# The shift's share of the keys as VectorE dot products with transposed key weights, and the shift's own products in pairs of k tiles

## Chip, cores and metric

One core of one Trainium2 chip. The metric is the device time of one launch in microseconds (us). The kernel before took a median of 1557.75 us over 3 runs (1557.66 to 1557.91).

## What is computed

One layer of a diffusion backbone on 256 latent tokens x and 256 context tokens ctx, 2048 features, all in float32. What matters here is the first half:

```
mod   = silu(c)     @ w_mod + b_mod          # shift, scale, gate, ... for x
mod_c = silu(c_ctx) @ w_mod + b_mod          # the same for ctx
h  = rms_norm(x,   g) * (1 + scale)   + shift
hc = rms_norm(ctx, g) * (1 + scale_c) + shift_c
q, k, v, gates = h @ w_in ;   k_c, v_c = hc @ w_in
```

There are ten key heads (eight of the neighbourhood mixer, two of the windowed one) of 128 features each. Attention, gates, branch and output projections, a second norm and a gated convolutional FFN follow. Because the shift is the same vector for all tokens of a stream, its share of a key head is one vector of 128 numbers per stream: shift @ w_k. The kernel makes the keys without the shift and adds that vector afterwards.

## The kernel before

All products are float32 products in two or three parts: a weight block of 1 MB (128 partitions x 2048) is loaded by `raw_block` (line 97) into one of four buffers of the tag "raw", and `halves` (line 116) splits it into `wh` on ScalarE (line 109) and `wl` on VectorE (line 113), two instructions each, into two buffers each. `block(ahead)` (line 144) hands out the next block of the stream, asks for the split of the block after it and for the loads of one or more further ones. The framework's scheduler lays out each engine's instructions in order of the program among those it holds ready, so a later load or product can be put ahead of an earlier one that isn't ready; once laid out, the order on an engine is fixed.

The stages around the change, in order:

- First sweep of the keys (lines 319 to 340): six key heads, sixteen k tiles, each used as soon as its scale column is there. At its end the sums are evacuated by VectorE, six instructions at line 340, and the accumulators become free.
- Second sweep (lines 345 to 363): the other four key heads. Ahead of the 24 key products of each k tile stand the products of the shift itself, silu(c) @ w_mod, in `pm` (line 354): four column tiles of 32 columns with 512 moving columns. Their weights `wm_sh` come through the four "raw" buffers, two tiles ahead, beside the key weights. Then ScalarE evacuates `pm` (line 365), TensorE transposes it (368), VectorE adds the bias to make the columns `shc` (373), and ScalarE and VectorE make the whole of h, hi and lo part, from the normalised input `xn` (lines 377 to 385). Then the pool that holds `xn` is closed (386).
- Values (lines 388 to 449): ten weight blocks, 576 products at line 428. Beside them `key_shift` (line 402) loads the key weights a second time, 640 KB for each k tile, and multiplies them with `shc` on TensorE, four column tiles per k tile, in `pc` (line 409). After the ninth block `pc` is evacuated, transposed (439) and copied, and 20 ScalarE instructions (445) add it to the keys. Also beside the values, thirteen modulation columns are made by `mods` (line 176): a load of 1 MB of `wm_b` and one VectorE dot product over 2048 columns (line 186), with the row silu(c) broadcast to all partitions in `crb` (line 189).
- Attention (lines 451 to 591): query blocks are made two heads ahead by `fill` (line 494), beside rotation, scores, softmax and values. The mask is in `bz` (line 395), which is loaded at the start of the values.
- Gates and branches (lines 593 to 636): one dot product beside most gates, and one more beside the branch block of j = 4 and j = 8 (line 623). The remaining six of the 48 modulation columns come beside the output projection.

Then come the output projection (line 640), the FFN (from line 773) and the down projection.

Of the kernel before, what the change touches and what calls it, by code (L numbers as in the profile page):

```python
# [15 lines left out]
P = 128  # L16
D = 2048
KT = D // P
S = 256
# [12 lines left out]
# columns of the packed per-feature vectors  # L32
# [10 lines left out]
# blocks of the weight stream, in the order of use  # L43
# [7 lines left out]
NK1 = 6  # key tiles of the first sweep  # L51
# [5 lines left out]
def layer_kernel(ctx, tc, xc, xt, ccol, crow, wm_sc, wm_sh, wm_b, cols, wk, ws, rope, mask_a, bias_b, out):  # L57
# [34 lines left out]
    ggd = tc.dram_tile([2, KT, P], F32, name="ggd")  # L92

# [3 lines left out]
    def raw_block(src, shape=(P, 2048)):  # L97
        nraw[0] += 1
        r = wp.tile([P, 2048], F32, tag="raw", bufs=4, name=f"raw{nraw[0]}")
# [25 lines left out]
    # the weight stream: loads run two or three blocks ahead, the splitting one  # L125
# [5 lines left out]
    raws, parts, nblk, place, queue, last = {}, {}, [0], {}, {}, []  # L131

    def load_to(i):
        for q in range(min(i, len(srcs) - 1) + 1):
            if q not in raws:
                raws[q] = raw_block(*srcs[q])
# [14 lines left out]
    def mm2(pt, wh, wl, act, k0, n, kk0, first, last, step=P, off=0):  # L151
        """accumulate n k-tiles; act is [P, kt, 2(hi, lo), 256]; result: two halves to be added"""
# [23 lines left out]
    def mods(n, row, ahead=1):  # L176
        """the next n modulation columns of x: one dot product per partition"""
# [11 lines left out]
    def silu_row(pool):  # L189
        r = pool.tile([P, D], F32, tag="crb", bufs=1, name=f"crb{nmod[0]}")  # L190
# [16 lines left out]
    def gain_dram(i, g):  # L207
        """as a row"""
# [9 lines left out]
    def keep_busy(n, nm):  # L218
        """products of constants: the tensor engine's clock falls when it waits for long"""
# [4 lines left out]
    # ================= mixers =================  # L224
    zs = ExitStack()
    with ExitStack() as mx:
# [3 lines left out]
        with ExitStack() as at:  # L230
# [3 lines left out]
            def rope_of(t, which, nm):  # L234
                """in place; the pairs of the rotation lie 64 partitions apart"""
# [10 lines left out]
            shc = hcp.tile([P, KT, 32], F32, name="shc")  # L246
# [11 lines left out]
            nc.gpsimd.memset(shc, 0.0)  # L258
            rsc = {}

# [11 lines left out]
            # (1 + b) g of the scale  # L272
# [71 lines left out]
            # the other keys, while the weights of the shift come in  # L344
            pm = bank("pmsh")
            pk = [acc(f"pk{NK1 + i}") for i in range(NK2)]
            rsh = {k: raw_block(wm_sh[k]) for k in range(2)}
            for g in range(4):
                wh, wl = block(1)
                for k in range(4 * g, 4 * g + 4):  # L350
                    if k + 2 < KT:
                        rsh[k + 2] = raw_block(wm_sh[k + 2])
                    for j in range(4):
                        nc.tensor.matmul(  # L354
                            pm[32 * j : 32 * j + 32, :], cc[:, k, :], rsh[k][:, 512 * j : 512 * j + 512],
                            start=k == 0, stop=k == KT - 1)
                    for v in range(2):
                        x_ = xn[:, k, v * S : v * S + S]
                        nc.vector.scalar_tensor_tensor(
                            out=x_, in0=x_, scalar=Gc[:, k, v : v + 1], in1=rs[:, v * S : v * S + S],  # L360
                            op0=ALU.mult, op1=ALU.mult)
                    for i in range(NK2):
                        keys(pk[i], wh, wl, (k % 4) * NK2 * P + i * P, k)
            ev = sp.tile([P, 512], F32, tag="hf", bufs=2, name="evsh")
            nc.scalar.activation(ev[:], pm[:], AF.Copy)
# [3 lines left out]
            # pt[p, b, 32 j + v] is the value of feature (4 j + b) * 128 + p  # L369
            view = pt[:].rearrange("p (b j w) -> p j b w", b=4, j=4, w=32)  # L370
            bm = col[:, C_BMOD : C_BMOD + KT].rearrange("p (j b) -> p j b", j=4)
            for v in range(2):
                nc.vector.tensor_tensor(
                    out=shc[:].rearrange("p (j b) w -> p j b w", j=4)[:, :, :, v],
                    in0=view[:, :, :, v], in1=bm, op=ALU.add)
            # the whole of h
# [17 lines left out]
            # what is added to the scores, and one row of zeros for the context  # L394
            bz = vp.tile([P, 7, S], F32, name="bz")
            crb = silu_row(cbp)
            sync.dma_start(out=bz[:, 0:2], in_=mask_a)
            nc.gpsimd.memset(bz[:, 6], 0.0)
            pc = bank("pc")
            nkc = [0]  # L400

            def key_shift(n):
                for _ in range(n):
                    k = nkc[0]
                    nkc[0] += 1
                    r = raw_block(wk[k], (P, KW))
                    for j in range(4):
                        n_ = min(384, KW - 384 * j)
                        nc.tensor.matmul(
                            pc[32 * j : 32 * j + 32, :n_], shc[:, k, :], r[:, 384 * j : 384 * j + n_],  # L410
                            start=k == 0, stop=k == KT - 1)

            nb = 0
            for c, (n0, nw, per) in enumerate(((0, 512, 4), (512, 512, 4), (1024, 256, 8))):
                pv = [acc(f"pv{c}_{i}") for i in range(4)]
                for g in range(KT // per):
                    wh, wl = block(2)
                    for kk in range(per):
                        if nb < 8 and kk % 2:
                            key_shift(1)  # L420
                        if kk in (0, 3, 6) and nb and (kk != 3 or nb > 7):
                            mods(1, crb[:])
# [9 lines left out]
                    if nb == 9:  # L432
                        ev = cbp.tile([P, 384], F32, tag="evk", name="evk")
                        nc.gpsimd.memset(ev, 0.0)
                        nc.scalar.activation(ev[:, :P], pc[:, :P], AF.Copy)
                        nc.scalar.activation(ev[:96, P:], pc[:96, P:384], AF.Copy)
                        pt = bank("ptk")
                        for b in range(3):
                            nc.tensor.transpose(pt[:, b * P : b * P + P], ev[:, b * P : b * P + P], ident[:])
                        kb = cbp.tile([P, 384], F32, tag="kb", name="kb")  # L440
                        nc.vector.tensor_copy(kb[:], pt[:, :384])
                        for i in range(NKVA + NHB):
                            for v in range(2):
                                o_ = (i % 3) * P + 32 * (i // 3) + v
                                nc.scalar.activation(
                                    kT[:, i, v * S : v * S + S], kT[:, i, v * S : v * S + S], AF.Identity, bias=kb[:, o_ : o_ + 1])
# [10 lines left out]
            # query blocks and the first gates are done beside the attention of earlier heads  # L457
# [36 lines left out]
            def fill(half):  # L494
                """half of the products of the next query (or gate) block"""
# [113 lines left out]
        for j in range(KT):  # L609
# [13 lines left out]
            mods(1 if j in (4, 8) else 0, crb[:])  # L623
# [63 lines left out]
    def rstd_tok(ss, r):  # L687
        """the sum of the first three parts is ready when the last part comes"""
# [9 lines left out]
    with ExitStack() as ys:  # L698
# [19 lines left out]
        # second norm: shift with its bias, gain times (1 + scale)  # L718
# [80 lines left out]
    # the first two pairs go k by k, as h2 comes  # L799
# [9 lines left out]
    # behind the products of a block: its halves are added before the next block but one is split,  # L809
    # the rest of its work comes after that  # L810
# [172 lines left out]
```

## Time and profile before

| | us |
|---|---|
| median of 3 runs | 1557.75 (1557.66 to 1557.91) |
| span of the profiled execution, first to last instruction | 1556.1 |
| TensorE busy | 1540.4 (99%) |
| VectorE busy | 1067.3 (69%) |
| ScalarE busy | 783.8 (50%) |
| end of the first sweep / of the second sweep / of the values | 102.4 / 165.9 / 296.6 |

The profiled execution shows its span and no other time of its own; the median lies 1.65 us above that span. Engines are PE (TensorE), PEld (its weight loads), DVE (VectorE), ACT (ScalarE), POOL (GpSimd) and SP (the queue that issues the loads). A line such as "L409" is a line of the kernel. Matmul records are pipelined, so a matmul that is shown as 0.40 us long may be followed by the next after 0.23 us: costs are read from one start to the next.

### The profile page before, as it was taken

Reading aid. Unit: us, or ns where it says so; the run is one execution under the profiler, and the core shown is the slowest. Engines: PE = TensorE matmul, PEld = TensorE weight load, DVE = VectorE, ACT = ScalarE, POOL = GpSimd, SP = SyncE. Lnnn points to the kernel's source line nnn. Section 1 sums busy time; section 2 is a strip of 40 time slices with the busy share of each in tenths; the row PEclk is TensorE's granted clock in tenths of the full one; section 3 lists DMA queues with packets and bytes.
Section 4 is the critical chain, followed back from the end, with each engine's and each line's share of the span. In section 5 each row is a group of like instructions: output and inputs, shape, how many; then the busy total and the mean of one; then the engine's idle time right before and its main releaser. Section 6 shows DMA issues by size and latency. Waiting matters only on the chain.

```text
span 1556.1 us, 22874 instructions
## 1 busy us (share of the span) xinstructions
PE 1540.4 (99%) x9181; PEld 1317.5 (85%) x9181; DVE 1067.3 (69%) x1611; ACT 783.8 (50%) x1291; POOL 23.8 (2%) x29
## 2 busy tenths in 40 slices
PE   8999999999999999999999999999999999999998
PEld 8987766989998888888888888888888888888886
DVE  3563633798878898887667878887888776444444
ACT  4431411677775454555467555555555554343332
POOL 2210000000000000000000000000000000000000
PEclk9999999999999999999999999999999999999999
DMA  9868787733337898887955666666666556555552
GB/s 371 324 263 324 261 316 266 270 114 138 136 145 295 319 344 329 327 303 281 366 191 197 241 238 244 243 226 234 244 244 229 204 190 254 206 189 190 189 189 81
DMA packets 58393, 377.97 MB, mean 243 GB/s; under 512 B 6384, under 2 KB 6448, under 8 KB 16176
## 3 DMA queue, kind: packets, MB, share of 16 engines
q1 hardware_dynamic: 57712, 375.47, 64.9%
q8 instruction: 72, 1.18, 0.3%
q10 hardware_dynamic: 576, 1.05, 0.2%
q14 instruction: 33, 0.27, 0.0%
HBM read 372.27 MB, written 4.22 MB: 242 GB/s over the span
## 4 chain that ended last, share of the span: by engine, by line
PE 97%; DMA 1%; ACT 1%; DVE 0%; POOL 0%; SPq 0%; issue 0%; DVEq 0%; POOLq 0%
PE pu L156 21%; PE py_d L653 16%; PE pu L157 11%; PE pv L428 7%; PE pk L311 7%; PE pg L156 7%; PE py_o L653 6%; PE pq L156 4%; PE pb L156 4%; PE pg L157 4%; PE pq L157 2%; PE pb L157 2%; PE po L564 1%; PE s L534 1%; PE pmsh L354 1%; PE pm L282 1%
## 5 line engine op out<-in xcount | busy, mean ns | idle before, releaser
L113 DVE TENSOR_TENSOR wl<-raw,wh 128x1024 fp32r<-128x1024 f32 (+2 forms) x470 | 555.6, 1210 | 334.8 <-ACT wh L109 324.0
L109 ACT ACTIVATE wh<-raw 128x1024 fp32r<-128x1024 f32 (+2 forms) x470 | 474.2, 1042 | 410.2 <-PE py_d L653 135.5
L156 PE MATMUL pu<-h,wh 128*128 128x512 f32 x1408 | 488.6, 390 | 0.0
L157 PE MATMUL pu<-h,wl 128*128 128x256 f32 x1408 | 396.8, 282 | 0.0
L156 PEld LDWEIGHTS pu<-h,wh 128*128 128x128 f32 x1408 | 264.3, 188 | 55.6 <-ACT h L768 0.3
L157 PEld LDWEIGHTS pu<-h,wl 128*128 128x128 f32 x1408 | 266.1, 189 | 0.1
L653 PE MATMUL py_d<-wh,ff 128*128 128x512 f32 x704 | 221.1, 395 | 0.0
L156 PE MATMUL pg<-hx,wh 128*128 128x512 f32 x464 | 161.5, 390 | 0.0
L653 PEld LDWEIGHTS py_d<-wh,ff 128*128 128x128 f32 x704 | 131.9, 187 | 32.2
L186 DVE SCALAR_TENSOR_TENSOR raw<-raw,crb 128x2048 f32<-128x2048 f32 x64 | 146.1, 2285 | 16.9 <-DMA raw<-in_wm_b_dram 12.4
L653 PE MATMUL py_d<-wl,ff 128*128 128x512 f32 x352 | 139.0, 395 | 0.0
L157 PE MATMUL pg<-hx,wl 128*128 128x256 f32 x464 | 130.8, 282 | 0.0
L161 ACT ACTIVATE half_u<-pu 128x256 f32<-128x256 f32 x88 | 33.5, 383 | 152.8 <-PE pu L157 152.8
L156 PE MATMUL pq<-hx,wh 128*128 128x512 f32 x304 | 108.4, 395 | 0.0
L156 PEld LDWEIGHTS pg<-hx,wh 128*128 128x128 f32 x464 | 87.1, 188 | 18.3
L156 PE MATMUL pb<-oab,wh 128*128 128x512 f32 x256 | 89.6, 392 | 0.0
L157 PEld LDWEIGHTS pg<-hx,wl 128*128 128x128 f32 x464 | 87.7, 189 | 0.0
L311 PE MATMUL pk<-hx,wh 128*128 128x256 f32 x320 | 85.5, 290 | 0.2 <-PE pmsh L354 0.2
L157 PE MATMUL pq<-hx,wl 128*128 128x256 f32 x304 | 85.6, 282 | 0.0
L311 PE MATMUL pk<-hc,wh 128*128 128x256 f32 x320 | 82.8, 281 | 0.0
L653 PE MATMUL py_o<-wh,zz 128*128 128x512 f32 x256 | 80.3, 395 | 0.0
L653 PEld LDWEIGHTS py_d<-wl,ff 128*128 128x128 f32 x352 | 66.0, 187 | 16.3
(177 smaller groups left out, 1994.1 us busy)
## 6 DMA issues: line engine op xcount, KB each, us to landing
raw<-in_ws_dram SPq DMA_DIRECT2D x222, 1024.0 KB, 4.8
raw<-in_wm_b_dram SPq DMA_DIRECT2D x64, 1024.0 KB, 4.8
raw<-in_wm_sc_dram SPq DMA_DIRECT2D x16, 1024.0 KB, 7.6
raw<-in_wm_sh_dram SPq DMA_DIRECT2D x16, 1024.0 KB, 6.4
raw<-in_wk_dram SPq DMA_DIRECT2D x16, 640.0 KB, 5.0
raw<-in_wk_dram SPq DMA_DIRECT2D x7, 768.0 KB, 5.6
raw<-in_wk_dram SPq DMA_DIRECT2D x4, 1024.0 KB, 5.9
crb<-sild SPq DMA_DIRECT2D x4, 1024.0 KB, 5.9
```

The lines of the kernel that those rows point to most:

```text
L109: a_ = nc.scalar.activation(hi, src, AF.Copy)
L113: v_ = nc.vector.tensor_tensor(out=lo, in0=src, in1=hi, op=ALU.subtract)
L156: nc.tensor.matmul(pt[:, :], wh[:, w], a, start=first and i == 0, stop=False, skip_group_check=True)
L157: nc.tensor.matmul(pt[:, :S], wl[:, w], a[:, 0], start=False, stop=last and i == n - 1, skip_group_check=True)
L161: a_ = nc.scalar.activation(t[:], pt[:, S:], AF.Copy)
L186: nc.vector.scalar_tensor_tensor(out=r, in0=r, scalar=1.0, in1=row, op0=ALU.mult, op1=ALU.mult, accum_out=modx[:, j : j + 1])
L282: nc.tensor.matmul(pm[32 * j : 32 * j + 32, :P], cc[:, q, :], r[:, q * P : q * P + P], start=q < 4, stop=q >= KT - 4)
L311: nc.tensor.matmul(pk[:, v * S : v * S + S], wt[:, w], hh[v][:, k, a], start=k == 0 and a == 0 and wt is wh and v == 0, stop=k == KT - 1 a ...
L354: nc.tensor.matmul(pm[32 * j : 32 * j + 32, :], cc[:, k, :], rsh[k][:, 512 * j : 512 * j + 512], start=k == 0, stop=k == KT - 1)
L428: nc.tensor.matmul(pv[i][:, :nw], src[:, k, a, t0 : t0 + P], wt[:, w], start=k == 0 and q == 0, stop=k == KT - 1 and q == 2)
L534: nc.tensor.matmul(s_ps[:], qs[hd][:, a, qt * P : qt * P + P], k_[:], start=q == 0, stop=q == 2)
L653: nc.tensor.matmul(py[t][:], act[:, k, a, t * P : t * P + P], wt[:, w], start=k == 0 and q == 0, stop=k == nk - 1 and q == 2)
```

## The change

Three things are changed (comments that were taken out are not shown):

1. The shift's products run two k tiles at a time. Four `wm_sh` loads are asked for at once, and the key weights of the second sweep (blocks 9 to 12) get one buffer of their own in the pool of `xn`. The bias is added on evacuation (a loaded row `brow`, on VectorE, in place of the ScalarE copy), the shift rows are written to DRAM (`shd`), and `shc` is copied from the transposes.
2. `key_shift` and all that hangs on `pc` are gone. In their place stand 20 dot products on VectorE (`beside`): for each of the ten key heads one load of transposed key weights `wkt` (1 MB) and one product for each of the two streams, with the shift row broadcast to all partitions (`shr`). Two ScalarE additions per head follow at once (`key_bias`). They run beside value blocks 2 to 7; after them come eleven modulation columns, whose row takes over the buffer of a shift row.
3. The mask's buffer `bz` is made and loaded after the values, and two modulation columns move to the branch blocks of j = 11 and j = 13.

```diff
+            home.update({q: sp for q in range(9, 13)})
...
-            rsh = {k: raw_block(wm_sh[k]) for k in range(2)}
...
+            rsh = {k: raw_block(wm_sh[k]) for k in range(4)}
+            for k in range(KT):
+                if k % 4 == 0:
+                    wh, wl = block(1)
+                if k % 2 == 0:
+
+                    for q in (k, k + 1):
+                        for j in range(4):
+                            nc.tensor.matmul(
+                                pm[32 * j : 32 * j + 32, :], cc[:, q, :], rsh[q][:, 512 * j : 512 * j + 512],
+                                start=q == 0, stop=q == KT - 1)
+                    for q in (k + 4, k + 5):
+                        if q < KT:
+                            rsh[q] = raw_block(wm_sh[q])
...
-            nc.scalar.activation(ev[:], pm[:], AF.Copy)
+            nc.vector.tensor_tensor(out=ev[:], in0=pm[:], in1=brw[:], op=ALU.add)
+            sync.dma_start(out=shd.rearrange("j w n -> (j w) n"), in_=ev)
...
+            shr = []
+            for v in range(2):
+                shr.append(cbp.tile([P, D], F32, tag="row", bufs=2, name=f"shr{v}"))
+                sync.dma_start(
+                    out=shr[v].rearrange("p (j n) -> p j n", j=4), in_=shd[:, v].partition_broadcast(P))
+            junk = cbp.tile([P, D], F32, name="junk")
+            kb = cbp.tile([P, NKVA + NHB, 2], F32, name="kb")
+            rkt = {0: raw_block(wkt[0])}
+            crb = [None]
+            nbeside = [0]
+
+            def key_bias(i):
+                for v in range(2):
+                    o_ = slice(v * S, v * S + S)
+                    nc.scalar.activation(kT[:, i, o_], kT[:, i, o_], AF.Identity, bias=kb[:, i, v : v + 1])
+
+            def beside(n):
                 for _ in range(n):
-                    k = nkc[0]
-                    nkc[0] += 1
-                    r = raw_block(wk[k], (P, KW))
-                    for j in range(4):
-                        n_ = min(384, KW - 384 * j)
-                        nc.tensor.matmul(
-                            pc[32 * j : 32 * j + 32, :n_], shc[:, k, :], r[:, 384 * j : 384 * j + n_],
-                            start=k == 0, stop=k == KT - 1)
+                    i, v = divmod(nbeside[0], 2)
+                    nbeside[0] += 1
+                    if i < NKVA + NHB:
+                        if v == 0 and i + 1 < NKVA + NHB:
+                            rkt[i + 1] = raw_block(wkt[i + 1])
+                        r = rkt[i]
+                        nc.vector.scalar_tensor_tensor(
+                            out=r if v else junk[:], in0=r, scalar=1.0, in1=shr[v][:], op0=ALU.mult, op1=ALU.mult,
+                            accum_out=kb[:, i, v : v + 1])
+                        if v:
+                            key_bias(i)
+                    else:
+                        if crb[0] is None:
+                            crb[0] = silu_row(cbp, "row", 2)
+                        mods(1, crb[0][:])
...
-                        if nb < 8 and kk % 2:
-                            key_shift(1)
-                        if kk in (0, 3, 6) and nb and (kk != 3 or nb > 7):
-                            mods(1, crb[:])
+
+                        if nb and kk < (3 if nb % 2 else 4):
+                            beside(1)
...
+            bzp = at.enter_context(tc.tile_pool(name="bzp", bufs=1, side="right"))
+            bz = bzp.tile([P, 7, S], F32, name="bz")
+            sync.dma_start(out=bz[:, 0:2], in_=mask_a)
+            nc.gpsimd.memset(bz[:, 6], 0.0)
...
-            mods(1 if j in (4, 8) else 0, crb[:])
+            mods(1 if j in (4, 8, 11, 13) else 0, crb[:])
```

The transposed weights and the bias row are laid out ahead of the launch: `o["wkt"] = np.concatenate([kb, ka], axis=1).T.reshape(NKVA + NHB, P, D)` and `o["brow"]`.

## Rows read from the trace of the kernel before

**Rows 1.** The page: engines' busy time, the chain by engine, the splits on VectorE.

```profile
PE 1540.4 (99%) x9181; PEld 1317.5 (85%) x9181; DVE 1067.3 (69%) x1611; ACT 783.8 (50%) x1291; POOL 23.8 (2%) x29
...
PE 97%; DMA 1%; ACT 1%; DVE 0%; POOL 0%; SPq 0%; issue 0%; DVEq 0%; POOLq 0%
...
L113 DVE TENSOR_TENSOR wl<-raw,wh 128x1024 fp32r<-128x1024 f32 (+2 forms) x470 | 555.6, 1210 | 334.8 <-ACT wh L109 324.0
```

**Rows 2.** Busy by stretch: span, then PE, PEld, DVE, ACT, POOL, clock, DMA share, GB/s.

```profile
18.00:30.00 12.00, 11.85 (x164) 11.04 (x166) 5.71 (x11) 6.77 (x13) 2.90 (x2) 1.00 0.97 388
182.00:297.00 115.00, 115.00 (x645) 87.22 (x644) 52.14 (x48) 32.58 (x54) 0.67 (x2) 1.00 0.79 295
297.00:312.00 15.00, 15.00 (x85) 12.93 (x84) 12.10 (x24) 11.70 (x18) 0.00 (x0) 1.00 0.57 216
540.00:560.00 20.00, 20.00 (x117) 17.67 (x117) 19.66 (x26) 10.95 (x17) 0.00 (x0) 1.00 0.96 370
```

**Rows 3.** TensorE in order of time around one of the key shift's products.

```profile
205.90 0.40 PE L428 MATMUL pv<-wh,hx 128*128 128x512 f32 x1
206.23 0.85 PE L409 MATMUL pc<-raw,shc 128*32 128x384 f32 x8
207.00 0.50 PE L428 MATMUL pv<-wh,hx 128*128 128x512 f32 x1
207.34 0.40 PE L428 MATMUL pv<-wl,hx 128*128 128x512 f32 x1
207.57 0.40 PE L428 MATMUL pv<-wh,hx 128*128 128x512 f32 x1
```

**Rows 4.** The tile pc: its products (start of the first and the last).

```profile
L409 PE MATMUL pc<-raw,shc x128: 272/486/510, 167.1 to 270.3; 128*32 128x384 f32 x96, 128*32 128x128 f32 x32
```

**Rows 5.** TensorE at the start of the values, and at the transposes of pc.

```profile
165.92 0.60 PE L368 MATMUL ptsh<-ident,evsh 128*128 128x128 f32 x4
167.08 0.85 PE L409 MATMUL pc<-raw,shc 128*32 128x384 f32 x8 [0.57 <-DVE shc L373]
168.34 0.50 PE L428 MATMUL pv<-wh,hx 128*128 128x512 f32 x1 [0.41 <-ACT hx L383]
...
284.93 0.49 PE L439 MATMUL ptk<-ident,evk 128*128 128x128 f32 x3
285.18 0.48 PE L428 MATMUL pv<-wh,hx 128*128 128x256 f32 x2
```

**Rows 6.** TensorE in the second sweep: the first shift products, then a later one.

```profile
102.48 2.78 PE L354 MATMUL pmsh<-raw,cc 128*32 128x512 f32 x24
105.41 0.36 PE L311 MATMUL pk<-hx,wh 128*128 128x256 f32 x1 [0.15 <-PE pmsh L354]
...
157.81 0.28 PE L311 MATMUL pk<-hc,wl 128*128 128x256 f32 x1
158.02 1.06 PE L354 MATMUL pmsh<-raw,cc 128*32 128x512 f32 x8
...
159.24 0.28 PE L311 MATMUL pk<-hc,wh 128*128 128x256 f32 x1
```

**Rows 7.** VectorE in order of time: dot products at the start and end of the values.

```profile
189.43 2.29 DVE L186 SCALAR_TENSOR_TENSOR raw<-raw,crb 128x2048 f32<-128x2048 f32 x1 [4.40 <-DMA crb<-sild]
191.65 0.08 DVE L186 DVE_READ_ACCUMULATOR raw<-raw,crb 128x1 f32 x1
...
293.06 2.29 DVE L186 SCALAR_TENSOR_TENSOR raw<-raw,crb 128x2048 f32<-128x2048 f32 x1
```

**Rows 8.** Loads issued from 182 to 297 us: count, KB each, median us to landing.

```profile
raw<-in_wm_b_dram SPq DMA_DIRECT2D x12, 1024.0 KB, 6.6
crb<-sild SPq DMA_DIRECT2D x1, 1024.0 KB, 6.9
```

**Rows 9.** SP's queue after the second sweep: the issue of the broadcast row silu(c).

```profile
182.45 0.42 SPq L191 DMA_DIRECT2D crb<-sild  x1
```

**Rows 10.** Waits from 300 to 312 us: us in total, times, longest.

```profile
ACT q L109 <- DVE rq L241: 1.4, 1, 1.4
```

More of the change, by code (lines that the diff above doesn't have):

```diff
@@ L56, in layer_kernel @@
 @with_exitstack
-def layer_kernel(ctx, tc, xc, xt, ccol, crow, wm_sc, wm_sh, wm_b, cols, wk, ws, rope, mask_a, bias_b, out):
+def layer_kernel(ctx, tc, xc, xt, ccol, crow, wm_sc, wm_sh, wm_b, cols, wk, wkt, ws, brow, rope, mask_a, bias_b, out):
     nc = tc.nc
@@ L92, in layer_kernel, with raw_block @@
     ggd = tc.dram_tile([2, KT, P], F32, name="ggd")
+    shd = tc.dram_tile([4, 32, 512], F32, name="shd")
     nraw = [0]
     nmod = [0]
-    def raw_block(src, shape=(P, 2048)):
+    def raw_block(src, shape=(P, 2048), pool=None):
         nraw[0] += 1
-        r = wp.tile([P, 2048], F32, tag="raw", bufs=4, name=f"raw{nraw[0]}")
+        r = (pool or wp).tile([P, 2048], F32, tag="raw", bufs=1 if pool else 4, name=f"raw{nraw[0]}")
         n = int(np.prod(shape[1:]))
@@ L130, in layer_kernel @@
     srcs += [(ws[i], (P, 2048)) for i in range(NBLK)]
-    raws, parts, nblk, place, queue, last = {}, {}, [0], {}, {}, []
+    raws, parts, nblk, place, home, queue, last = {}, {}, [0], {}, {}, {}, []
     def load_to(i):
@@ L135, in load_to @@
             if q not in raws:
-                raws[q] = raw_block(*srcs[q])
+                raws[q] = raw_block(*srcs[q], pool=home.get(q))
     def split_to(i):
@@ L187, in mods, with silu_row @@
                 out=r, in0=r, scalar=1.0, in1=row, op0=ALU.mult, op1=ALU.mult, accum_out=modx[:, j : j + 1])
-    def silu_row(pool):
-        r = pool.tile([P, D], F32, tag="crb", bufs=1, name=f"crb{nmod[0]}")
+    def silu_row(pool, tag="crb", bufs=1):
+        r = pool.tile([P, D], F32, tag=tag, bufs=bufs, name=f"crb{nmod[0]}")
         sync.dma_start(out=r, in_=sild.rearrange("a b -> (a b)").partition_broadcast(P))
@@ L345, in layer_kernel @@
             pm = bank("pmsh")
+            brw = sp.tile([P, 512], F32, tag="sq", bufs=2, name="brw")
+            sync.dma_start(out=brw, in_=brow)
             pk = [acc(f"pk{NK1 + i}") for i in range(NK2)]
-            rsh = {k: raw_block(wm_sh[k]) for k in range(2)}
[L348 to L352, printed above, removed]
-                    for j in range(4):
-                        nc.tensor.matmul(
-                            pm[32 * j : 32 * j + 32, :], cc[:, k, :], rsh[k][:, 512 * j : 512 * j + 512],
-                            start=k == 0, stop=k == KT - 1)
[L357 to L363, printed above, removed]
@@ L364, in layer_kernel @@
-            ev = sp.tile([P, 512], F32, tag="hf", bufs=2, name="evsh")
-            nc.scalar.activation(ev[:], pm[:], AF.Copy)
+            rsh = {k: raw_block(wm_sh[k]) for k in range(4)}
[12 more added lines that the diff above has]
+                for v in range(2):
+                    x_ = xn[:, k, v * S : v * S + S]
+                    nc.vector.scalar_tensor_tensor(
+                        out=x_, in0=x_, scalar=Gc[:, k, v : v + 1], in1=rs[:, v * S : v * S + S],
+                        op0=ALU.mult, op1=ALU.mult)
+                for i in range(NK2):
+                    keys(pk[i], wh, wl, (k % 4) * NK2 * P + i * P, k)
@@ L431, in layer_kernel @@
                     nb += 1
[L432 to L446, printed above, removed]
                 for i in range(4):
@@ L928, in _layout @@
     o["wk"] = np.concatenate([kb, ka], axis=1).reshape(KT, P, KW)
+    o["wkt"] = np.concatenate([kb, ka], axis=1).T.reshape(NKVA + NHB, P, D)
+    o["brow"] = np.zeros((P, 512), w_mod.dtype)
+    for v in range(2):
+        o["brow"][v::32] = f(b_mod)[0][:2048].reshape(4, 512)
     def slabs(w, n):
```

24 lines of the change are left out of this document (7 added, 17 removed).

## Prediction

> **What bounds the kernel now.** I read the page's busy times and chain first: TensorE is busy for 99% of the span and 97% of the chain that ended last runs through it, so what is taken off TensorE shortens the run one for one, until another engine or the loads are late [rows 1]. The busy times by stretch come second. While the values run, from 182 to 297 us, TensorE has no idle time, VectorE works 52.1 of 115 us, and the loads move 295 GB/s, 33.9 MB in all [rows 2]. In the first 15 us of attention VectorE works 12.1 of 15 us: little is free there [rows 2]. The granted clock is 1.00 (2.4 GHz) in all these stretches. Then I read TensorE's instructions in order of time around each thing that the change removes, and VectorE's around one dot product.
>
> The sum is made against the profiled execution (span 1556.1 us) and carried over to the median, 1.65 us above it.
>
> **Removed: the key shift on TensorE.** Value products follow each other every 0.233 us (207.34 to 207.57). Around one product of the key shift, three of them start at 205.90, 207.00 and 207.34; without it the third would start at 205.90 + 2 x 0.233 = 206.37, so one k tile of the key shift costs 0.97 us [rows 3]. There are 128 instructions of it, 8 for each of the 16 k tiles [rows 4]. The first costs nothing: it runs at 167.08 in a gap in which the values wait for ScalarE's hx until 168.34 [rows 5]. So 15 x 0.97 = 14.6 us. The transposes of pc cost 0.25 us by the next product's start and 0.49 at most [rows 5]. I take 14.9 us. The other end is 16.3: the values last 128.3 us (168.34 to 296.62), and 384 products of 512 columns at 0.233 plus 192 of 256 at half of that would last 112.0.
>
> **Changed: the shift's own products in pairs.** In the second sweep a product of the keys follows the last every 0.117 us (256 columns, half of the 0.233). The third start after the shift's product is 159.24 instead of 157.81 + 0.233, so a single k tile costs 1.2 us; three k tiles in a row take 105.41 - 102.48 = 2.9 us [rows 6]. The slope is therefore 0.9 us for each further tile and a pair costs 2.1, where two singles cost 2.4. Before, one group of three and 13 singles stand there. If the scheduler begins with one pair, the accumulators that are free only at 105.41 make TensorE wait for the rest, and seven pairs replace 13 singles: 15.6 - 14.7 = 0.9 us won. If it begins with two pairs, they end 0.9 us later and six pairs remain: 15.6 - 12.6 - 0.9 = 2.1 us. I take 1.1. The bias row, the evacuation on VectorE in place of ScalarE and the write to DRAM are hidden: behind the last pair stand 48 key products (5.6 us), where behind the last single there were 24. The one buffer for key weights asks for its next load when the last block is split, four k tiles (some 15 us) ahead of its use, while a load takes about 7 us [rows 8]. If that cover went, the sweep would wait a few microseconds at one block.
>
> **Added: 20 dot products on VectorE.** One takes 2.22 us from start to start, the accumulator's read in it [rows 7]. Two columns leave the stage, so 18 x 2.22 = 40 us come, less the copy of pc (0.6). VectorE then works 52.1 + 39.4 = 91.5 us in a stretch of 115 - 15 = 100 us [rows 2]. That fits only if it seldom waits. But the shift rows are written into memory of the closed pool, as crb before, which was issued at 182.45 and was there at 189.43 [rows 7, 9]; with two rows instead of one and no mask beside them I take the same 7 us, during which VectorE is idle for 5 us (the split of one block fills the rest). And the row silu(c) now comes into the buffer of a shift row: its load is issued after the 19th dot product, lands 6.9 us later [rows 8], and the 20th covers 2.2 of them: 4.7 us. Together 101 us of 100. Up to there no product waits: a block of values lasts 48 x 0.233 = 11.2 us and asks VectorE for 3.5 x 2.22 and a split of 2 x 1.21 [rows 1], 10.2 us, the split of the next block having a block's time of lead.
>
> **Moved behind that: eleven columns in a row.** The 20th dot product ends about 189.4 + 20 x 2.22 + 5 splits x 2.4 + some 1 = 247 us; the row silu(c) is there at 251.4. From then on VectorE uses up 1 MB every 2.2 us, and the loads can't follow: 370 GB/s over 20 us and 388 over 12 us are the longest high stretches I find [rows 2], and 1.049 MB at 370 GB/s are 2.83 us. Fourteen loads (11 columns, three weight blocks), two of them in when the row lands: 251.4 + 12 x 2.83 + 2.2 = 287.6 for the end of the last column. The values end at 296.6 - 14.9 = 281.7 (the 1.1 of the pairs shifts both). So VectorE is 5.9 us late. Before, its last column ended at 295.3, 1.3 us ahead of the values' end [rows 7], and even so ScalarE waited 1.4 us for the rotated query [rows 10]. How much of the 5.9 TensorE sees depends on the fixed order on VectorE: if only the split of the second query block stands behind the columns (5.9 + 2.4, against 16 x 0.35 = 5.6 us of query products), 2.7 us; if rotation, key and value splits do too, all 5.9 and the 1.3 that were in hand before, 7.2. I take the middle, 5.0 us. The bounds are 0 (four loads ahead and a better order) and far more (below).
>
> The Trainium skill's page "DMA: Bandwidth & Descriptors", section Specifications, speaks against this change in the same place: it gives a limit of about 358 GB/s per core on the HBM side. The rows show 388 GB/s over 12 us, so here the measurement decides [rows 2]. By the page a load would take 2.93 us and the sum would come out 1.2 us higher.
>
> **Other edits.** The two columns moved to j = 11 and 13 cost nothing: from 540 to 560 us, where j = 4 has such an extra column, TensorE works 20.00 of 20 us with VectorE at 19.7 [rows 2]. The 20 ScalarE additions to the keys are spread instead of standing at the stage's end; I count nothing; a gain from it is within the upper end of 16.3. On POOL two clears vanish and that of bz moves; nothing is queued behind it. On SP the mask's load now stands at the values' end and waits for memory of the values' small pool. If that is held until the last column, the loads of query blocks behind it come late too; the third query block starts 11.2 us after the values' end and needs 6.6 us of load and 2.4 of split, so nothing is lost below a lateness of 2.2 us, and beyond it no more than the lateness that is counted already.
>
> **Sum:** 14.9 + 1.1 - 5.0 = 11.0 us off: 1557.75 - 11.0 = **1546.7**; for the likeliest case 1543 to 1550.
>
> **Rivals.** *All is hidden.* The loads run at 388 and further ahead, and the scheduler puts splits and rotations between late columns. For it: VectorE waits for data, so other ready work can go first. Against: 101 us of work in 100. 1557.75 - 16.0 = 1541.7, with the upper ends 1539.4.
> *Most is given back.* Each load takes 3.5 us, because a buffer is held until its dot product is done and only four exist: 251.4 + 42 + 2.2 = 295.6, 13.9 us late, of which TensorE sees 12.9 by the same middle: 1554.6. For it: a column's load landed after 6.6 us (median), with two on the way 3.3 us each [rows 8].
> *Slower.* The same place, the ring of four buffers, with one load on the way half of the time: 5 us each, 251.4 + 60 + 2.2 is 32 us late, TensorE waits 31: 1557.75 - 16 + 31 = 1573. It decides from 3.8 us per load on: then the last column is 17 us late and the gain is gone. Against: from 540 to 560 us the same ring and the same dot products ran at 370 GB/s [rows 2].
> *It doesn't do what it says:* pairs may change nothing if the scheduler lays out groups as it did with the first three; that costs at most the 1.1.
>
> **How the numbers follow.** Forecast 0.47, all hidden 0.27, most given back 0.18, slower 0.08. A measurement of this kernel tells some 0.2%, 3.1 us. Forecast, hidden and about half of "given back" are faster by more: 0.83; same 0.09; slower 0.08. The range leaves out the slower case and the far ends: 1540 to 1556.
>
> **What would show it.** Right: no L409 and no pc on TensorE, pairs of 16 instructions about 2.1 us apart from their neighbours, value blocks of 11.2 us without a gap, the values' end near 281 us, VectorE above 90% from 182 to 281, waits of VectorE for wm_b in the last 30 us of the values, and a TensorE gap of about 5 us between 285 and 300. Wrong: gaps inside the first eight value blocks (shift rows or splits late), a clock below 1.00 after 285, or query blocks that wait for ws.

## The result, and the profile after

The changed kernel takes 1551.49 us (median of 5 runs, 1545.13 to 1551.67) against 1557.91 (1557.66 to 1558.11) for the kernel before, measured beside it: a ratio of 0.9946 [0.9934, 0.9957] (in brackets the 95% interval). Measured a second time it took 1549.03 (1546.49 to 1550.76), ratio 0.9945 [0.9932, 0.9959]. So it is faster by about 0.55%, 2 to 5 us slower than the forecast of 1546.7, and inside the range. It also spreads over 4 to 6.5 us, where the kernel before spreads over 0.5. The profiled execution is the fastest one, 1545.13 us with a span of 1543.0.

Busy times and chain of the page after (before: [rows 1]):

```profile
PE 1524.3 (99%) x9050; PEld 1316.5 (85%) x9050; DVE 1111.7 (72%) x1651; ACT 784.6 (51%) x1288; POOL 23.0 (1%) x27
...
PE 89%; DVE 6%; DMA 3%; issue 1%; ACT 1%; SPq 0%; POOL 0%; DVEq 0%; POOLq 0%; ACTq 0%
```

TensorE is busy 16.1 us less, but the span is 13.1 shorter: 3 us are new waits, and VectorE and the loads now have 9% of the chain. TensorE in order of time shows where (start, duration, what, and in brackets the idle time before it and its releaser):

```profile
102.41 2.76 PE L358 MATMUL pmsh<-raw,cc 128*32 128x512 f32 x18
...
110.90 1.92 PE L358 MATMUL pmsh<-raw,cc 128*32 128x512 f32 x14
...
164.38 0.60 PE L376 MATMUL ptsh<-ident,evsh 128*128 128x128 f32 x4
166.79 0.73 PE L449 MATMUL pv<-wh,hx 128*128 128x512 f32 x2 [1.81 <-ACT hx L389]
...
215.06 0.73 PE L449 MATMUL pv<-wh,hc 128*128 128x512 f32 x2 [0.60 <-ACT vv L454]
...
280.57 0.39 PE L157 MATMUL pq<-hx,wh 128*128 128x512 f32 x1
...
293.38 1.66 PE L545 MATMUL s<-k,q 128*128 128x512 f32 x6 [1.56 <-ACT q L110]
296.68 0.38 PE L158 MATMUL pq<-hx,wl 128*128 128x256 f32 x1 [1.41 <-DVE wl L114]
```

The second sweep ends at 164.38 where it ended at 165.92 [rows 5]: 1.54 us from the pairs. The values wait as long as before for hx (2.41 us from the sweep's end to the first product; 2.42 in [rows 5]), but before, a product of the key shift stood in that wait, and now TensorE is idle for 1.81 us of it. The values last from 166.79 to 280.57, 113.8 us where they lasted 128.3: 14.5 us from the key shift, with a wait of 0.60 near 215 in it. Behind the values come two waits of 1.56 and 1.41, together 2.97; from the values' end to the last instruction it is 1262.4 us where it was 1259.5, 2.95 us more. The sum is -1.54 - 14.5 + 2.95 = -13.1, the difference of the spans.

VectorE in order of time shows what the last two wait for:

```profile
189.18 2.29 DVE L425 SCALAR_TENSOR_TENSOR junk<-raw,shr 128x2048 f32<-128x2048 f32 x1 [6.44 <-issue]
...
195.96 2.29 DVE L425 SCALAR_TENSOR_TENSOR raw<-raw,shr 128x2048 f32<-128x2048 f32 x1 [2.14 <-DMA shr<-shd]
...
245.76 2.28 DVE L425 SCALAR_TENSOR_TENSOR raw<-raw,shr 128x2048 f32<-128x2048 f32 x1
...
253.29 2.29 DVE L187 SCALAR_TENSOR_TENSOR raw<-raw,crb 128x2048 f32<-128x2048 f32 x1 [0.68 <-DMA crb<-sild]
...
269.61 2.29 DVE L187 SCALAR_TENSOR_TENSOR raw<-raw,crb 128x2048 f32<-128x2048 f32 x1 [2.39 <-DMA raw<-in_wm_b_dram]
...
282.83 2.36 DVE L114 TENSOR_TENSOR wl<-raw,wh 128x1024 fp32r<-128x1024 f32 x2 [1.33 <-ACT wh L110]
...
287.32 2.29 DVE L187 SCALAR_TENSOR_TENSOR raw<-raw,crb 128x2048 f32<-128x2048 f32 x1
289.54 0.08 DVE L187 DVE_READ_ACCUMULATOR raw<-raw,crb 128x1 f32 x1
289.72 0.43 DVE L163 TENSOR_TENSOR rq<-pq,half_q 128x256 f32<-128x256 f32 x1
...
293.37 0.43 DVE L114 TENSOR_TENSOR q<-rq,q 128x256 fp32r<-128x256 f32 x1 [0.48 <-ACT q L110]
```

The last column ends at 289.6, 9 us behind the values. The rotation of the first head's query and the splits of its keys and values stand behind it on VectorE; then ScalarE splits the query, and the scores start at 293.38. TensorE doesn't wait all that time: the split of the second query block (282.83) stands ahead of the last two columns, so two query blocks (11.25 us from 280.57) cover all but 1.56 us. The stretches (busy time of PE, PEld, DVE, ACT, POOL; clock, DMA share, GB/s) say what holds the columns:

```profile
182.00:281.00 99.00, 98.40 (x518) 83.38 (x517) 85.82 (x80) 32.60 (x52) 0.00 (x0) 1.00 0.84 306
246.00:281.00 35.00, 35.00 (x247) 32.64 (x246) 30.57 (x30) 10.77 (x18) 0.00 (x0) 1.00 0.97 369
```

In the last 35 us the DMA engines are busy for 97% and move 369 GB/s, which is the rate of [rows 2] that the forecast took. And the tile of the shift rows gives a landing that it didn't foresee, 14.4 us for the second where crb took 6.9 [rows 8]:

```profile
DMA to landing us min/median/max: 8.0/11.2/14.4
```

ScalarE near 214 us shows the wait inside the values. An addition to the keys waits for its dot product, and two copies that free accumulators stand behind it:

```profile
214.02 0.51 ACT L415 ACTIVATE kT<-kT,kb 128x256 f32<-128x256 f32 x1 [3.12 <-DVE raw L425]
214.43 1.07 ACT L454 ACTIVATE vv<-pv 128x512 f32<-128x512 f32 x2
```

### The profile page after: what moved, and what is told of

Its sections match the earlier page's. It is cut to its first block, busy times and chain, and to the rows that moved or that the text cites. A ratio compares the mean times of both kernels' runs of the same rounds, so it can differ in the third digit from the quotient of the medians.

```text
span 1543.0 us, 22636 instructions
## 1 busy us (share of the span) xinstructions
PE 1524.3 (99%) x9050; PEld 1316.5 (85%) x9050; DVE 1111.7 (72%) x1651; ACT 784.6 (51%) x1288; POOL 23.0 (1%) x27
## 4 chain that ended last, share of the span: by engine, by line
PE 89%; DVE 6%; DMA 3%; issue 1%; ACT 1%; SPq 0%; POOL 0%; DVEq 0%; POOLq 0%; ACTq 0%
PE pu L157 21%; PE py_d L664 16%; PE pu L158 11%; PE pk L312 7%; PE pg L157 7%; PE py_o L664 6%; PE pq L157 4%; PE pb L157 4%; PE pg L158 4%; PE pq L158 2%; PE pb L158 2%; PE po L575 2%; PE s L545 1%; DVE wl L114 1%; DVE junk L425 1%
```

## Experiments

A hole is a wait of TensorE. Theory T1: the change gives time back where TensorE idles, near 166 us and near 293 and 297 us, because the last columns are late, and again where its clock falls behind such a hole. Its rivals are named T2 in each expectation. All times are medians of 4 or 5 runs; ratios are to the kernel before.

**The changed kernel again.** No edit.

> The changed kernel as it is, once more, to see how often its span is near 1543 us and how often near 1549.5, and where the two differ. T1 (the last columns end 9 us behind the values, the rotated query and the last query weights come late, TensorE has two holes near 293 and 297 us of 3 us together, and where the granted clock falls behind them up to 6.5 us more are lost): most times near 1551.5, some near 1545; a profile of a long execution shows a granted clock below 1.00 just behind 293 us, and one of a short execution shows 1.00 there. T2 (the clock falls elsewhere, for instance behind the 1.8 us hole at the values' start near 166 us): the same times, but the low clock stands behind 166 us or at the end of the run.

Its times stand above. In the profile (1546.49 us) the holes are 1.8 us near 166, and 2.8 and 1.4 near 295 and 298. The clock stood by stretches of 1 us:

```profile
165.00:166.00 1.00, 0.02 (x1) 0.00 (x0) 1.00 (x4) 1.00 (x2) 0.00 (x0) 1.00 1.02 426
166.00:167.00 1.00, 0.17 (x1) 0.17 (x2) 1.00 (x2) 1.00 (x3) 0.00 (x0) 1.00 1.01 426
167.00:168.00 1.00, 1.00 (x4) 0.49 (x4) 1.00 (x2) 1.00 (x4) 0.00 (x0) 0.78 0.74 311
168.00:169.00 1.00, 1.00 (x3) 0.63 (x3) 1.00 (x4) 1.00 (x3) 0.00 (x0) 0.50 0.49 74
169.00:170.00 1.00, 1.00 (x4) 0.81 (x3) 1.00 (x4) 1.00 (x4) 0.00 (x0) 0.50 0.62 172
170.00:171.00 1.00, 1.00 (x4) 0.72 (x3) 1.00 (x4) 1.00 (x3) 0.00 (x0) 0.51 0.98 418
171.00:172.00 1.00, 1.00 (x6) 0.82 (x5) 1.00 (x3) 1.00 (x4) 0.00 (x0) 1.00 0.93 393
```

TensorE idled from 165 to 166.8; then its granted clock fell to 0.50 (1.2 GHz) although it worked without a break, and came back. By these rows 0.22 + 0.50 + 0.50 + 0.49 = 1.7 us are lost. T1 put the fall behind 293 us, T2 behind 166: here T2's place was right. In the first profile neither place shows a fall.

**No columns beside the last value block.**

```diff
-                        if nb and kk < (3 if nb % 2 else 4):
+                        if 0 < nb < 9 and kk < (3 if nb % 2 else 4):
-            mods(1 if j in (4, 8, 11, 13) else 0, crb[:])
+            mods(1 if j in (4, 6, 8, 10, 11, 12, 13) else 0, crb[:])
```

> The columns that stood beside the last value block are moved into attention (three more extra columns at j = 6, 10 and 12), so that the splits of keys, queries and values and the last query weights stand on VectorE ahead of nothing late. T1: both holes near 293 and 297 us are gone, 3 us less than the changed kernel's best, and no execution loses clock there: 1541 to 1543 us, all within 1.5 us of each other. T2 (the low clock comes from elsewhere): the holes are gone but the times stay spread, some near 1542 and most near 1548. If attention has no room on VectorE for three more columns of 2.2 us, each shows as a hole of up to 2 us where it stands: 1545 to 1548.

1551.09 us (1549.49 to 1551.56), 0.9954 [0.9942, 0.9967]: T1's time missed. The holes near 293 us did shrink (1.0 ahead of the scores, 0.3 for query weights), but TensorE in order of time shows something neither theory had:

```profile
759.97 2.62 PE L223 MATMUL busy<-ident,ones 128*128 128x128 f32 x22
```

And TensorE's waits (us in total, times, longest):

```profile
PE ptx L769 <- DVE r L700: 4.9, 1, 4.9
```

The 33 products that fill the next norm's wait depend on nothing, and the scheduler laid them among the gates and into the output projection (eleven of them here, two records each). There they took TensorE's time, the norm's wait of 4.9 us lay open, and the clock fell behind it (0.50 from 802 to 804 us). This run judges that move, not the columns.

**The same, with the filling products held in place.**

```diff
-        keep_busy(33, "2")
+        with tc.issue_after(last[0]):
+            keep_busy(33, "2")
```

(last[0] is the output projection's last product.)

> As the kernel without columns beside the last value block, with the 33 filling products of the next norm held behind the last product of the output projection, where the changed kernel has them (in the run without late columns the scheduler had laid them into the output projection, where they took TensorE's time and left the norm's wait open). T1: the holes near 293 and 297 us are below 1 us each, the norm's wait is filled again: 1541 to 1543 us, and up to 2 us more where the clock falls behind the values' start. T2 (the columns in attention cost what they save): 1544 to 1549 us.

1545.77 us (1545.46 to 1547.69), 0.9926 [0.9914, 0.9939]: 5.3 us less than without the hold, but in the range of T2 and 0.8 us above T1's 1545. The profiled execution, the longest of the five, lost 1.7 us of clock behind 166 us. The shortest, at a mean clock of 0.999, is still 2.5 us above T1's 1543. Besides the hole near 166, the profile has waits of 0.75 (for a query weights' split), 0.99 and 0.58 (for queries) between 288 and 304 us, 0.68 near 216, and 1.2 at the products pb of the branch blocks, where the moved columns stand: the last is what T2 said.

**Shift rows in one piece.**

```diff
-    shd = tc.dram_tile([4, 32, 512], F32, name="shd")
+    shd = tc.dram_tile([32, 4, 512], F32, name="shd")
-            sync.dma_start(out=shd.rearrange("j w n -> (j w) n"), in_=ev)
+            for j in range(4):
+                sync.dma_start(out=shd[:, j], in_=ev[32 * j : 32 * j + 32, :])
-                    out=shr[v].rearrange("p (j n) -> p j n", j=4), in_=shd[:, v].partition_broadcast(P))
+                    out=shr[v], in_=shd[v].rearrange("j n -> (j n)").partition_broadcast(P))
```

> Each shift row is written to DRAM so that its 2048 values lie in one piece of 8 KB, and is read as one piece to every partition, in place of four pieces of 2 KB. If the pieces made the two rows late (8.0 and 14.4 us from issue to landing, 6.9 for the row silu(c) that is one piece): both land within about 8 us, the 2.1 us wait of VectorE near 196 us goes, the last column ends 2 to 6 us earlier, the holes near 293 and 297 us shrink from 3 us to below 1.5: 1543 to 1549 us. If the bytes alone set the landing (two rows of 1 MB): no change, 1545 to 1551.5.

1547.43 us (1543.91 to 1549.91), 0.9932 [0.9918, 0.9945]. The tile of the shift rows in its profile:

```profile
DMA to landing us min/median/max: 5.4/6.4/7.4
```

And TensorE at the first scores:

```profile
295.02 2.93 PE L546 MATMUL s<-k,q 128*128 128x512 f32 x6 [2.58 <-ACT q L110]
```

The rows now land in 5.4 and 7.4 us, and the dot products start 2.6 us earlier. But the last column ends at 291.2, as in the second profile of the changed kernel: VectorE waits 4.3 us for columns' loads (2.8 and 5.2 in the two profiles of the changed kernel), and the holes of 2.6 and 0.8 us near 295 and 299 are not below 1.5 as T1 had it. The clock fell in this profile behind 166 and again behind 293 us. The interval overlaps that of the changed kernel, so a gain is not shown.

**Single k tiles again.**

```diff
-                if k % 2 == 0:
+                if True:
-                    for q in (k, k + 1):
+                    for q in (k,):
```

> Undoes the pairing alone: the shift's own products come one k tile at a time again, in the order of the kernel before. The forecast's price of the pairs was 1.1 us (0.9 to 2.1), the two profiles say 1.5: the second sweep is 0.9 to 2.1 us longer and the whole run 1546 to 1553 us. If pairs bring nothing, the sweep is as long as in the changed kernel.

1549.38 us (1547.87 to 1551.85), 0.9947 [0.9935, 0.9960]. The values' first product comes at 169.12 instead of 166.79, 2.3 us later, a little above the range; 14 groups stand behind the first, where the kernel before has 13. The median doesn't show it: it is drowned in the spread.

**First k tiles of the input ahead of a split.**

```diff
+                if k == 1:
+                    queue[14] = (a_.ins, v_.ins)
+                    split_to(14)
```

(a_ and v_ are the last ScalarE and VectorE instructions of those tiles.)

> The first k tiles of the shifted input go ahead of a weight block's split on ScalarE and VectorE, which shortens the 2.4 us that the values wait between the end of the second sweep and their first product (2.0 us of it is one half of the split on ScalarE). T1 (work ends where TensorE is free; both holes open the way to a low clock): the hole of 1.8 us near 166 us shrinks below 0.6, no low clock stands behind it, the values start 1.2 to 1.8 us earlier; but the last columns are set by the loads and not by the values' start, so the hole near 293 us grows by about as much: 1543 to 1549 us, less than 1 us better at its best. T2 (columns follow the values' start): the 1.2 to 1.8 us stay, 1541 to 1547 us.

1546.46 us (1546.05 to 1547.23), 0.9930 [0.9916, 0.9943]. The values start at 165.96, 0.83 us earlier (1.2 to 1.8 were expected), with a hole of 0.97 and no fall behind it. Of the 0.83 us a wait of 1.6 for a copy near 214 takes 0.5 back, and the scores wait longer:

```profile
295.53 2.96 PE L548 MATMUL s<-k,q 128*128 128x512 f32 x6 [4.03 <-ACT q L110]
```

The clock fell behind this wait. What is won ahead of the columns is given back later, as T1 had it; but the time lies in the ranges of both theories.

**Both holes filled.** Eight products of the identity behind the shift's transposes, and eight ahead of the first scores:

```diff
+            with tc.issue_after(tr.ins):
+                keep_busy(8, "v")
...
+            with tc.issue_after(m_):
+                keep_busy(8, "s")
```

(tr is the last of the transposes, m_ the last query product ahead of the scores.)

> The changed kernel with eight products of the identity (1.8 us) laid into each of the two waits of TensorE: behind the transposes of the shift (near 165 us) and ahead of the first scores (near 293 us). They compute nothing that is used. No work is moved, so at an even clock the time is that of the changed kernel's best, 1543 to 1545 us. T1 (idle TensorE lets its clock fall): the granted clock stays 1.00 near 167 and 295 us in the profile, the times lie within 2 us of each other, 1543 to 1545.5 us. T2 (the clock falls for another reason): times spread from 1545 to 1551.5 us as before.

1547.82 us (1546.97 to 1550.45), 0.9941 [0.9929, 0.9954]: the spread stayed, 3.5 us. In the profile the clock is 1.00 behind both filled holes, and fell in a third place, behind a wait of 1.9 us for a copy:

```profile
164.57 1.95 PE L225 MATMUL busy_v<-ident,ones 128*128 128x128 f32 x16
...
217.00:218.00 1.00, 1.00 (x4) 0.74 (x3) 0.97 (x3) 1.00 (x3) 0.00 (x0) 0.50 0.65 229
218.00:219.00 1.00, 1.00 (x4) 0.81 (x3) 1.00 (x1) 1.00 (x2) 0.00 (x0) 0.50 1.03 410
```

Two other runs had spans of 1545.0 and 1548.3, both at a mean clock of 0.999. So the waits themselves differ from run to run, by 3.3 us here. T1 holds for the clock in this one profile; the times are T2's.

**Additions to the keys behind the copies.**

```diff
-                            key_bias(i)
+                            pend.append(i)
...
+                with tc.issue_after(e_.ins):
+                    for _ in range(len(pend) if c else 3):
+                        key_bias(pend.pop(0))
```

> In the changed kernel ScalarE's additions to the keys stand between the copies that empty the values' accumulators: near 214 us one addition waits 3.1 us for its dot product, two copies stand behind it, and TensorE waits 0.6 us for an accumulator (0 to 1.9 us in the profiles so far). Here six additions stand behind the first column group's copies and fourteen behind the second's. T1 (ScalarE's queue is a third place that gives time back): no wait for a copy near 215 us in the profile, ScalarE no longer idle for a dot product ahead of a copy; 0.5 to 2 us off the median of the changed kernel, 1547 to 1550 us, the holes near 166 and 293 us as they were. T2 (only the two known holes matter): 1549 to 1551.5 us.

1549.78 us (1547.95 to 1551.77), 0.9949 [0.9937, 0.9961]. There is no wait near 215 us in its profile (nor in the second one of the changed kernel), and no time won: the scores wait 3.4 us and the query weights 1.8, more than in the changed kernel's. The time lies in the ranges of both theories; the gain that T1 expected is not shown.

**No loads for eleven columns.**

```diff
-                        mods(1, crb[0][:])
+                        nmod[0] += 1
+                        nc.vector.scalar_tensor_tensor(
+                            out=junk[:], in0=junk[:], scalar=1.0, in1=crb[0][:], ...
```

> Leaves out the loads of the eleven columns of the modulation that stand beside the values (11 MB); their dot products run on a buffer that is there already, so those eleven columns are not computed. VectorE's work stays. If the loads set the end of the last column (the forecast's step: 2.83 us for each load where a dot product takes 2.22): the columns follow each other without a wait, the last ends 6 to 10 us earlier, at 280 to 284 us, the holes near 293 and 297 us fall below 1 us together, and the time is 1540 to 1544 us (up to 1.7 us more where the clock falls behind 166 us). If VectorE's work alone sets it: the last column still ends near 289 us and the time stays at 1545 to 1551 us.

1542.74 us (1541.82 to 1543.73), 0.9904 [0.9889, 0.9919]. First and last column on VectorE:

```profile
254.38 2.29 DVE L434 SCALAR_TENSOR_TENSOR junk<-junk,crb 128x2048 f32<-128x2048 f32 x1 [1.10 <-DMA crb<-sild]
...
282.25 2.29 DVE L434 SCALAR_TENSOR_TENSOR junk<-junk,crb 128x2048 f32<-128x2048 f32 x1
```

And the wait for the scores that is left, from TensorE's waits:

```profile
PE s L550 <- ACT q L110: 0.5, 1, 0.5
```

The columns begin 1.1 us later than in the changed kernel, follow each other without a wait for data and end at 284.5, 5 us earlier (a little less than expected), and both holes near 293 and 297 us go. The hole near 166 is still there, 2.3 us in this profile, with a fall of the clock behind it. VectorE's work is all there: the loads set the end of the last column.

**All edits together:** rows in one piece, no late columns, first k tiles ahead, filling products in place (the four diffs above).

> All together: shift rows in one piece of 8 KB, no columns beside the last value block, the first k tiles of the shifted input ahead of a split, the filling products of the norm held in place. T1 (two holes and the clock behind them are all that the change gives back): holes below 0.6 us near 166 us and below 1 us near 293 us, clock 0.998 or more, 1538.5 to 1541 us with a spread below 1.5 us. T2 (a third place gives time back): 1542 to 1549 us, with a hole elsewhere.

1542.07 us (1541.80 to 1542.13), 0.9899 [0.9886, 0.9913]: faster than both kernels, with a spread of 0.3 us and a clock of 0.999. TensorE's waits from the values on:

```profile
PE pv L453 <- ACT hx L390: 1.0, 1, 1.0
PE pb L157 <- ACT wh L110: 0.9, 2, 0.4
...
PE s L549 <- ACT q L110: 0.6, 1, 0.6
...
PE pb L158 <- DVE wl L114: 0.3, 1, 0.3
```

The time is 1 us above T1's; the spread and the clock are T1's. The first hole is 1.0 instead of the 0.6 expected, and the columns that were moved to the branch blocks cost 1.2 us at their products pb.

**All edits but the rows in one piece** (that diff taken back).

> The kernel with all edits together, but with the shift rows in four pieces of 2 KB again. By itself the edit took the landing from 8.0 and 14.4 us to 5.4 and 7.4 and moved nothing at the values' end. If the rows matter once the late columns are gone: dot products begin 2 to 3 us later, the query weights' splits come later, holes near 293 us of 0.5 to 2 us are back, 1542.5 to 1545 us. If not: 1541.8 to 1542.3 us, as with all edits.

1543.79 us (1543.38 to 1544.07), 0.9910 [0.9896, 0.9923]: 1.7 us more, but not at 293 us, where the wait is the same 0.6:

```profile
213.86 0.73 PE L452 MATMUL pv<-wh,hc 128*128 128x512 f32 x2 [1.69 <-ACT vv L457]
```

Late rows make late dot products, these late additions, and these late copies. With the late columns gone, nothing behind gives this wait back.

**All edits, and the additions behind the copies** (that diff on top).

> All edits together, and the additions to the keys behind the copies. In the profile of all edits together no copy was late, so this can only help where ScalarE's weight splits stood behind an addition: 1541 to 1542.3 us. If fourteen additions in a row (7 us) hold up a weight split, a hole of up to 2 us near 262 us: 1542.5 to 1544 us.

1542.04 us (1541.82 to 1542.13), 0.9899 [0.9885, 0.9912]: the same, as expected, since no copy was late in that kernel.

## Why the prediction was right, and where it was off

| step | forecast | measured |
|---|---|---|
| key shift off TensorE | 14.9 us, at most 16.3 | 14.5, waits included; the values last 112.4 us with all edits, so 15.9 without them |
| pairs | 1.1 (0.9 to 2.1) | 1.54 |
| first dot product, last one's end | 189.4, 247 | 189.2, 248.0 |
| first column | 251.4 | 253.3 |
| last column's end, values' end | 287.6, 281.7 | 289.6, 280.6 |
| seen by TensorE | 5.0 (2.7 to 7.2) | 3.0; 3.4 to 5.2 in the second profile and in the variants with the same columns |
| additions on ScalarE | 0 | 0.6 (0 to 1.9) |
| clock behind the holes | 0 | 0, or 1.7 each time it falls |

**The mechanism was right.** TensorE's share went as forecast; the pairs came out between the two layouts named (the first group holds 18 products, two tiles and a part). VectorE does the 20 dot products and eleven columns beside the values (busy for 87% from 182 to 281 us, where above 90% was named). Eleven columns behind the 20th dot product are late, and the run without their loads shows that it is the loads. Their rate was right too: 369 GB/s are 2.84 us for each load of 1.049 MB, against 2.83, and from the start of the first column to the end of the last it is 36.3 us, against 36.2. The rival *most is given back* (3.5 us each) and *slower* (5 us) did not come. The page "DMA: Bandwidth & Descriptors" of the Trainium skill, section Specifications, has about 358 GB/s as the limit, worked out as half of what two cores share; 369 GB/s over 35 us, with one core running, stand in the rows above, so here too the measurement decides.

**The lateness was larger, and TensorE saw less of it.** With the 1.1 of the pairs taken off, the forecast's marks are 188.3, 246, 250.3 and 286.5 for VectorE and 280.6 for the values' end. The values ended there, but VectorE was 1, 2, 3 and 3 us behind: the last column is 9.0 us late, not 5.9, and all of the difference arose ahead of the first column. A part of it is the second shift row, which landed after 14.4 us where 7 were taken; no run shows a gain from mending that alone (rows in one piece: the last column is no earlier), because the columns' loads are waited for then.

**Three steps failed, and two errors offset each other.** The first is the choice between two orders on VectorE, of which "the middle, 5.0 us" was taken. By these orders a lateness of 9.0 us would cost 5.8 or 10.3. Neither came: the second query block's split stands ahead of the last two columns (282.83), two query blocks cover 11.25 us, and TensorE saw 3.0. So it is luck that 5.0 is as near as it is: the lateness was 3 us too small and the share of it that TensorE sees too large. The fastest execution, in whose values and attention the clock didn't fall, lies 1.6 us below the forecast (1545.13).

The second is the sentence that the first product of the key shift "costs nothing: it runs at 167.08 in a gap". It took no time, but it kept TensorE working; with it gone the idle time there is 1.81 instead of 0.57 + 0.41 us [rows 5], and in some executions the clock falls. The forecast took the clock of 1.00 over from [rows 2] and listed a fall behind 285 as a sign that it was wrong; falls behind 166 or 293 us stand in seven of the nine profiles in which one of these two holes is open, and in none of the four profiles with 0.97 us near 166 does it fall behind that. Eight products laid into the wait kept the clock at 1.00 there in the one profile taken. For the runs without a profile the mean clocks give an estimate. Three of the first five executions have 0.995 and spans of 1549.5 to 1549.7, where the profiled one has 0.998 and 1543.0: 0.003 of 1549.5 us is 4.6 us of the 6.5 (3 to 6, since the clock is known to three places). Of the second five one has 0.995 and 1548.8, where the profiled one has 0.997 and 1544.6: 3.1 of 4.2 us by the same reckoning. So most of the spread, and of the 2 to 5 us by which the medians are above 1546.7, is the clock's; the rest is the run-to-run length of the waits, which the filled holes show by themselves.

The third is "I count nothing" for the spread additions on ScalarE: they stand on ScalarE, waiting for dot products, ahead of copies that TensorE needs (214.02), and TensorE waits 0.6 us near 215, a gap inside the first eight value blocks, which the forecast had among its signs of being wrong.

**"All is hidden"** was priced at 1541.7; the kernel with all edits, in which three of the eleven columns stand elsewhere, takes 1542.07. The price fits, though its terms differ (15.9 for the key shift and 1.5 for the pairs, less the waits that are left). What kept the change from it is where the last columns and the work around them stand, not VectorE's share of the keys.

## What to carry to other kernels

When work is taken off the engine that bounds a kernel, look at what it covered there: a product that ran for nothing in a wait may have held the clock, and a wait without it can cost more than its length. Where loads bound a stretch, time won ahead of it is given back at its end, so first move loads out of it (here three columns of 1 MB), and then mend the waits ahead (here 1.7 us from the rows in one piece, which alone had shown no gain). After any edit, see whether work without dependences, such as filling products, still stands where it was.

## What was not expected of the hardware

- **The clock behind short holes.** TensorE's granted clock fell to 0.50 behind idle times of 1.8 to 4.9 us and came back after a loss of 1.7 us, in some executions and not in others with the same hole (1.8 us near 166: 1.00 in the first profile, 0.50 in the second; 2.8 us near 295: 1.00 in the second). The kernels that leave no such hole have mean clocks of 0.998 to 0.999 and spreads of 1.1 us at most, the kernel before among them. The Trainium skill's page "TensorE: Matmul & The Clock Gate", section "HAM oscillation — how this bites in real kernels", says that waits for data between groups of products set the array back to the lower clock and that the next products then start slow. The rows agree in that; the waits drawn there are longer, some 3 to 5 us, than the 1.8 us behind which the clock fell here.
- **A broadcast row in pieces of 2 KB.** Two rows of 8 KB, read to all 128 partitions in pieces of 2 KB, landed in 8.0 and 14.4 us (7.7 to 9.3 and 14.2 to 15.6 in the other profiles with such pieces); in one piece of 8 KB in 5.4 and 7.4, and in 6.9 and 8.9 in the kernel with all edits. The skill's page "DMA: Bandwidth & Descriptors", section "Why small descriptors are slow (HBM only)", has a fixed overhead of about 3 cycles for each packet, with 32 bytes a cycle: an estimate from it is 3 of 67 cycles, 4.5%, for a piece of 2 KB. The rows show far more. The place of the pieces in DRAM changed with their size, and the two were not told apart.
